# Merge gate projections by seven block products in place of eight

## The chip, the cores and the metric

One core of one Trainium2 chip runs the kernel. The metric is the device time of one execution in microseconds (us). Arithmetic is in float32; every large matmul is made of three, since both operands are split into a high part (float32r) and the rest: high by high, low by high, high by low.

## The reference

Two layers over 512 tokens of width 1024 (H is the normed input of 512 x 1024). Each layer projects H by one wide matrix, feeds four token mixers, gates them and merges them:

```python
merge = merge_in.reshape(B, T, N_BRANCH, D_MODEL)
...
    branch = (o * jax.nn.silu(gates[:, :, i])) @ w_branch[i]
    term = jax.nn.sigmoid(merge[:, :, i]) * branch
    acc = term if acc is None else acc + term
return x + acc @ w_out
```

merge_in is H times a 1024 x 4096 slice of the input weights: four 1024 x 1024 gate matrices, one per branch i.

## The kernel before

Tensors lie feature-major: 128 features on partitions, 512 tokens along the free dimension. `dense` (L224) makes one projection of 128 output features: 24 matmuls, for eight input blocks k of 128 features and three operand parts, with a 128 x 128 piece of weights as the stationary operand and 512 tokens as the moving one, into one of three PSUM banks named d. Its result is taken out of PSUM by a small generator that joins the list `bg` and is stepped on at every second matmul.

Weights come through the class `Stream` (L84) in one fixed order, 80 tiles of 128 x 1024 (512 KB) per layer. SP issues the loads into three buffers wr; `Stream.split` (L112) makes the high part on ACT (L69) into wh and the low part on DVE (L70) into wl, two buffers each, one tile ahead of the matmuls. A buffer wr is loaded again as soon as it is split.

A layer goes in these stages. First the key, query and value projections (`v_group`, L476, has tokens as rows: a block of H is stationary there and 400 columns of weights move). Then the eight branch gates (`GATES`, SiLU on ACT, L863), with the compressed-key work between. Then attention: 12 `Unit`s (L569), each of four score blocks S (L585, L586, softmax L588 to L600), transposes T (L609) and products PV (L630), written out by hand over 57 steps s (L920, L921). `FILL` = 7 matmuls of a filler (L890) are traced at each step: 16 projections of 24 matmuls, the last four being the merge gates of output block 0. Then the merge, eight output blocks m of 128 features (L942): for each, four dense projections give the gate logits of the four branches (L258 multiplies by the token's 1/rms, L749 takes tanh of half of it, since sigmoid(z) = (1 + tanh(z/2))/2), and `branches` (L753) makes four products of six matmuls (L764) into banks s and pt, multiplies by 1 + tanh (L769), adds (L773) and splits the sum (L72, L73) as a moving operand for the output projection. At last eight dense projections by w_out (L956 adds the residual; in the second layer they are made in two token halves of 256, L979).

The order in which an engine works is not the source order alone: Tile's scheduler takes, for each engine, the instruction that its own time model says is ready, with the source order as the priority, and allots buffers by tag (t: 8, st: 20, y: 16, p: 5, ptc: 2, V: 1) as they come free. The order so made is fixed in the program; each engine then runs its list in order.

## Time and profile before

| | |
|---|---|
| median of 3 runs | 974.78 us (974.34 to 974.78) |
| profiled execution | 972.54 us |
| its span, first to last instruction | 970.8 us |
| TensorE busy | 951.2 us, 98% of the span |
| VectorE (DVE) busy | 654.9 us, 67% |
| ScalarE (ACT) busy | 460.7 us, 47% |
| DMA traffic | 100.61 MB, mean 104 GB/s |

PE is TensorE's matmuls, DVE is VectorE, ACT is ScalarE, SP the queue that issues most DMAs. A matmul's record is longer than its share of the engine, since matmuls are pipelined: the pace is read from starts that follow each other. A row with "x96" is that many instructions merged. Releaser names after "<-" say what ended an idle time.

### The profile page before, as it was taken

What the parts mean: (1) busy time and instruction counts of PE and PEld (TensorE: products, weight loads), DVE (VectorE), ACT (ScalarE), POOL (GpSimd) and SP (SyncE); (2) the same over time, 40 slices, a digit from 0 to 9 for tenths busy, and PEclk for the clock granted to TensorE, in tenths of its full rate; (3) what the DMA queues carried; (4) which work ended last, traced back from release to release, by engine and by line L of the source; (5) the groups of instructions that cost most, each with busy time, mean ns of one, the idle gap of its engine ahead of it and who ended that gap; (6) DMA issues with size and microseconds to landing.
All of it is one profiled execution on the core that took longest, in us unless ns stands there. A gap on an engine that the chain in (4) does not pass through costs nothing.

```text
span 970.8 us, 12716 instructions
## 1 busy us (share of the span) xinstructions
PE 951.2 (98%) x4792; PEld 809.7 (83%) x4792; DVE 654.9 (67%) x1297; ACT 460.7 (47%) x816; POOL 17.2 (2%) x29
## 2 busy tenths in 40 slices
PE   7999999999999999999999999999999999999996
PEld 5988888888878888888889888888887888888896
DVE  6695699978775555446668549998779544555565
ACT  7384575666533232323426637566654332323363
POOL 0000000000000000000100000000000000000011
PEclk9999999999999999999999999999999999999998
DMA  6253232131122322335424322221210323232553
GB/s 264 76 177 106 87 98 66 56 98 51 59 86 89 100 97 92 103 111 182 163 66 155 130 87 86 67 69 62 66 65 23 129 87 109 87 109 87 185 185 129
DMA packets 31836, 100.61 MB, mean 104 GB/s; under 512 B 3600, under 2 KB 5664, under 8 KB 31776
## 3 DMA queue, kind: packets, MB, share of 16 engines
q1 hardware_dynamic: 30240, 96.65, 30.3%
q0 software_dynamic: 672, 2.11, 0.5%
q10 hardware_dynamic: 864, 1.05, 0.3%
q8 instruction: 37, 0.61, 0.3%
q14 instruction: 23, 0.19, 0.1%
HBM read 95.60 MB, written 4.19 MB: 103 GB/s over the span
## 4 chain that ended last, share of the span: by engine, by line
PE 96%; DVE 2%; ACT 0%; DMA 0%; issue 0%; POOL 0%; DVEq 0%; ACTq 0%; POOLq 0%
PE ps_d L237 73%; PE ps_s L764 4%; PE ps_pt L764 4%; PE ps_o L630 3%; PE ps_pt L609 3%; PE ps_s L488 2%; PE ps_pt L488 2%; PE ps_s L586 2%; PE ps_s L585 1%; PE ps_o L349 1%; DVE t L769 1%; DMA ng<-in_gains_dram 0%; PE ps_o L171 0%; PE ps_o L473 0%; PE ps_o L199 0%
## 5 line engine op out<-in xcount | busy, mean ns | idle before, releaser
L237 PE MATMUL ps_d<-xh,wh 128*128 128x512 f32 x888 | 349.1, 393 | 7.6 <-ACT xh L72 6.7
L237 PE MATMUL ps_d<-xl,wh 128*128 128x512 f32 x888 | 348.9, 393 | 0.0
L69 ACT ACTIVATE wh<-wr 128x1024 fp32r<-128x1024 f32 (+2 forms) x160 | 166.7, 1044 | 329.6 <-issue 221.3
L237 PE MATMUL ps_d<-xh,wl 128*128 128x512 f32 x888 | 241.2, 391 | 0.0
L70 DVE TENSOR_TENSOR wl<-wr,wh 128x1024 fp32r<-128x1024 f32 (+2 forms) x160 | 192.7, 1205 | 54.2 <-ACT wh L69 44.5
L237 PEld LDWEIGHTS ps_d<-xh,wh 128*128 128x128 f32 x888 | 167.5, 189 | 41.1 <-ACT xh L72 6.7
L237 PEld LDWEIGHTS ps_d<-xl,wh 128*128 128x128 f32 x888 | 167.3, 188 | 34.0 <-DVE xl L73 1.2
L237 PEld LDWEIGHTS ps_d<-xh,wl 128*128 128x128 f32 x888 | 165.7, 188 | 33.2
L258 DVE TENSOR_TENSOR t<-ps_d,rstd 128x512 f32<-128x512 f32 x106 | 73.0, 688 | 153.5 <-PE ps_d L237 153.0
L237 PE MATMUL ps_d<-st,wh 128*128 128x256 f32 (+1 forms) x384 | 67.6, 319 | 0.8 <-ACT wh L69 0.8
L590 ACT ACTIVATE p<-p,nm 128x128 f32<-128x128 f32 (+1 forms) x96 | 53.3, 556 | 31.1 <-DVE nm L588 30.8
L237 PEld LDWEIGHTS ps_d<-st,wh 128*128 128x128 f32 x384 | 57.1, 190 | 6.1 <-ACT wh L69 1.0
L588 DVE CUSTOM_DVE_ANT_0 p<-ps_s,cst 128x128 f32<-128x128 f32 (+1 forms) x96 | 45.4, 485 | 14.3 <-PE ps_s L586 9.1
L69 ACT ACTIVATE pth<-ps_pt 128x384 fp32r<-128x384 f32 (+1 forms) x72 | 37.1, 522 | 27.1 <-PE ps_pt L609 13.2
L70 DVE TENSOR_TENSOR ptl<-ps_pt,pth 128x384 fp32r<-128x384 f32 (+1 forms) x72 | 42.3, 596 | 2.7 <-ACT pth L69 2.6
L609 PE MATMUL ps_pt<-cst,p 128*128 128x128 f32 x240 | 40.8, 276 | 1.9 <-DVE ptl L70 1.2
L764 PE MATMUL ps_pt<-y,wh 128*128 128x512 f32 x128 | 41.6, 391 | 0.0
L764 PE MATMUL ps_s<-y,wh 128*128 128x512 f32 x128 | 40.8, 396 | 0.6 <-DVE y L643 0.6
L749 ACT ACTIVATE t<-t 128x512 f32<-128x512 f32 x64 | 39.4, 615 | 1.7 <-DVE t L258 1.5
L237 PE MATMUL ps_d<-st,wl 128*128 128x256 f32 (+1 forms) x192 | 37.9, 319 | 0.0
L630 PE MATMUL ps_o<-pth,V 128*128 128x256 f32 x144 | 37.3, 275 | 0.4 <-DVE o L654 0.4
L630 PE MATMUL ps_o<-ptl,V 128*128 128x256 f32 x144 | 36.1, 292 | 0.6 <-DVE ptl L70 0.6
(230 smaller groups left out, 1080.5 us busy)
## 6 DMA issues: line engine op xcount, KB each, us to landing
wr<-in_w_all_dram SPq DMA_DIRECT2D x159, 512.0 KB, 3.3
t<-in_xT_dram SPq DMA_DIRECT2D x16, 256.0 KB, 4.1
wr<-in_w_all_dram SPq DMA_DIRECT2D x8, 400.0 KB, 3.0
x1d<-t POOLq DMA_DIRECT2D x8, 256.0 KB, 2.3
xh<-x1d SPq DMA_DIRECT2D x8, 256.0 KB, 5.4
out_dram<-xh SPq DMA_DIRECT2D x12, 128.0 KB, 4.5
par<-in_par_dram SPq DMA_DIRECT2D x2, 279.5 KB, 4.7
wr<-in_w_all_dram ACTq DMA_DIRECT2D x2, 256.0 KB, 4.1
```

The costliest lines, as they stand in the source:

```text
L69: ACT.activation(hi, src, AF.Copy)
L70: DVE.tensor_tensor(lo, src, f32(hi), ALU.subtract)
L237: PE.matmul(acc[:, :width], w, r[k][:, tok], start=(n == 0), stop=(n == 23))
L258: DVE.tensor_tensor(t, acc, state["rb"], ALU.mult)
L488: PE.matmul(accs[tt][:, 0:400], x[:, tt * 128:tt * 128 + 128], w, start=(k == 0 and a == 0), stop=(kp == 3 and kk == 1 and a == 2))
L586: PE.matmul(s[:, :n], q2[:, c], kl[:, :n], start=False, stop=True)
L588: DVE.tensor_tensor_reduce(out=P[:, :n], in0=s[:, :n], in1=bias, scale=1.0, scalar=3e38, op0=ALU.add, op1=ALU.min, accum_out=nm)
L590: ACT.activation(P[:, :n], P[:, :n], AF.Exp, bias=nm, scale=-1.0, accum_out=sm)
L609: PE.transpose(p[:, c:c + 128], self.P[qt][:, kb * 128:kb * 128 + 128], ident)
L630: PE.matmul(dst, V[:, kb, self.vset, :], part[:, src], start=(self.fresh and self.cmp is None and b == 0 and kb == 0 and j == 0), stop=(se ...
L749: ACT.activation(t, t, AF.Tanh, scale=0.5)
L764: PE.matmul(p, w[:, c], r, start=(n == 0), stop=(n == 5))
```

## The change

The 512 x 1024 H is cut into two halves of tokens and two of input features, the gate weights of two branches (one half fh of 512 output features) into two halves of input features and the two branches. That 2 x 2 by 2 x 2 block product is made by seven products of sums and differences of blocks (P1 to P7, Strassen's scheme in Winograd's form) in place of eight. Each product is of 256 tokens by 512 input features by 512 output features: two halves h, two token blocks tt, two blocks kk, three parts, so 24 matmuls, now with a 128 x 128 block of H stationary and 512 weight columns moving. There are four such blocks per layer (fh, bp). The 1/rms goes into the tanh as a scale per partition, since tokens are rows now. P1, P6, P5 and P3 add up in banks X (d), P7 and P4 in W (s), P2 in Y (pt); partial sums are copied out of X by ACT between the products.

`combine_h` makes the sums of the blocks of H from the layer's input, loaded again; six of its 24 pieces are traced in the last attention steps, the rest ahead of the first P7. `prepare` makes the sums of the weight tiles on DVE and splits them; T2 is kept from P7 to P4. The stream now loads 80 merge tiles per layer (18 + 2 in each block, some twice) in place of 40, and has seven slots in the merge (three wr, the rope tables' buffer, three in V's buffer) in place of three. Sets of split weights rotate over wh/wl (two) and the buffers of the attention transposes (one), so three sets. The branch products have tokens as rows too. The merged sum of a half fh is transposed back by 16 PE transposes and split. Four of the eight SiLU gates move into the filler, made by tanh, in the place of the four merge gates; the compressed-key work moves from the gate stage to the attention's head; the filler is spread evenly over all 57 steps in place of 7 per step.

The diff, cut to its core (removed: `ev_merge`, `branches` and the loop over m, printed above; cut here too: buffer renames and the packing of the weights on the host):

```diff
-FILL = 7
 HID = (9, 11, 13, 15)
-GATES = [(0, 0), (2, 0), (0, 1), (2, 1), (1, 0), (3, 0), (1, 1), (3, 1)]
+GATES = [(0, 0), (2, 0), (0, 1), (2, 1)]
+GATES2 = [(1, 0), (1, 1), (3, 0), (3, 1)]
 BIG = 1e30
 HEAD_ROWS = (1, 3, 0, 2)
 SWAP = [(i + 8) % 16 if i < 16 else i for i in range(32)]
@@ -81,40 +82,85 @@
...
 
+
+    PRODUCTS = ("P1", "P2", "P7", "P6", "P5", "P3", "P4")
+
+    NEEDS = {"P1": (0,), "P2": (2,), "P7": (3, 1), "P6": (0,), "P5": (1, 0), "P3": (3,), "P4": (2,)}
...
-            self.order = [(l, i) for l in range(L) for i in range(NTILE)]
+            self.order = []
+            for l in range(L):
+                self.order += [(l, i) for i in range(MERGE0)]
+                for b in range(4):
+                    o = MERGE0 + 10 * b
+                    for name in PRODUCTS:
+                        self.order += [(l, o + 2 * q + h) for h in range(2) for q in NEEDS[name]]
+                    self.order += [(l, o + 9), (l, o + 8)]
+                self.order += [(l, i) for i in range(NTILE - KT, NTILE)]
...
+            self.slots = ["wr"] * 3
...
+    def combine_h(l):
+
+        src = xT.rearrange("(k p) t -> k p t", p=128) if l == 0 else x1d
+        H = T // 2
+        S = state["S"] = {n: [] for n in ("P7", "P6", "P5", "P3")}
+        lo_, hi_ = slice(0, H), slice(H, T)
+        keep = []
+        for k in range(4):
+            xa = [sb([128, T], "ptc", 2) for _ in range(2)]
+            for n in range(2):
+                nc.sync.dma_start(xa[n], src[k + 4 * n])
+            if k % 2 == 0:
...
+            yield
...
+            for n in range(2):
+                ACT.activation(xa[n], xa[n], AF.Copy, scale=ng[:, 8 * l + k + 4 * n:8 * l + k + 4 * n + 1])
+            yield
+            c = k % 2
...
+            DVE.tensor_tensor(tmp[:, 0], xa[0][:, lo_], xa[0][:, hi_], ALU.subtract)
+            DVE.tensor_tensor(s1[:, c], xa[0][:, hi_], xa[1][:, hi_], ALU.add)
+            parts("P7", tmp[:, 0])
+            yield
+            DVE.tensor_tensor(tmp[:, 1], s1[:, c], xa[0][:, lo_], ALU.subtract)
+            parts("P6", tmp[:, 1])
+            yield
+            s4 = xa[1][:, lo_]
+            DVE.tensor_tensor(s4, s4, tmp[:, 1], ALU.subtract)
+            parts("P3", s4)
+            yield
...
+        for k in range(4):
+            h, lo = xh[k][:, hi_], xl[k][:, hi_]
+            split(h, lo, keep[k // 2][:, k % 2])
+            S["P5"].append((h, lo))
+            yield
...
+    def prepare():
...
+        def parts(r):
+            if next(count) % 3 == 2:
+                hi, lo = (sb([128, 2, T], "ptx", 2, F32R).rearrange("p a b -> p (a b)") for _ in range(2))
             else:
...
+                hi, lo = sb([128, 1024], "wh", 2, F32R), sb([128, 1024], "wl", 2, F32R)
+            split(hi, lo, r)
+            ready.append((hi, lo))
...
+        for blk in range(4):
+            t2 = [None, None]
+            for name in PRODUCTS:
+                for h in range(2):
+                    r, slot = t2[h] if name == "P6" else ws.next_raw()
+                    if name in ("P7", "P5", "P6"):
+                        b, other = ws.next_raw()
+                        DVE.tensor_tensor(r, r, b, ALU.add if name == "P6" else ALU.subtract)
+                        ws.free(other)
+                        yield
+                    elif name == "P4":
+                        b, other = t2[h]
+                        DVE.tensor_tensor(r, r, b, ALU.subtract)
+                        ws.free(other)
+                        yield
+                    parts(r)
+                    if name in ("P7", "P6"):
+                        t2[h] = r, slot
+                    else:
+                        ws.free(slot)
+                    yield "ready"
...
+
+        rth = sb([128, 4], "rth", 1)
+        DVE.tensor_scalar(rth, state["rt"], 0.5, None, op0=ALU.mult)
+        big = sb([128, 3, 1024], "V", 1)
+        ws.slots += ["rope"] + [big[:, n] for n in range(3)]
+        ws.fill()
...
+        for fh in range(2):
+            acc = [None] * 4
+            for bp in range(2):
+                X = Y = W = None
+                sig = {}
+                s1, u2, u4 = [None] * 2, [None] * 2, [None] * 2
+                for name in PRODUCTS:
+                    if name == "P1":
+                        X = [psum("d", 3) for _ in range(2)]
+                    elif name == "P2":
+                        Y = [psum("pt", 2) for _ in range(2)]
+                    elif name == "P7":
+                        run(side)
+                        W = [psum("s", 2) for _ in range(2)]
+                    bank = Y if name == "P2" else W if name in ("P7", "P4") else X
+                    opens = name in ("P1", "P2", "P7")
+                    for h in range(2):
+                        wh, wl = take_ready()
+                        for tt in range(2):
+                            for kk in range(2):
+                                k = 2 * h + kk
+                                a, b = rows(name, k, tt)
+                                d = slice(kk * 512, kk * 512 + 512)
+                                for n, (x, w) in enumerate(((a, wh), (b, wh), (a, wl))):
+                                    PE.matmul(bank[tt], x, w[:, d], start=(opens and k == 0 and n == 0),
+                                              stop=(name in ("P2", "P3", "P4") and k == 3 and n == 2),
+                                              skip_group_check=True)
+                            if h == 0 and tt == 0:
+                                merge_ahead(2)
+                        merge_ahead(2)
+                    for tt in range(2):
+                        if name in ("P1", "P6", "P5"):
+                            t = sb([128, T], "p", 5) if name == "P5" and bp == 0 else temp()
+                            ACT.activation(t, X[tt], AF.Copy)
+                            {"P1": s1, "P6": u2, "P5": u4}[name][tt] = t
+                        if name == "P2":
+                            DVE.tensor_tensor(s1[tt], Y[tt], s1[tt], ALU.add)
+                            tanh(s1[tt], s1[tt], tt)
+                            sig[0, tt] = s1[tt]
+                        elif name == "P5":
+                            DVE.tensor_tensor(u4[tt], W[tt], u4[tt], ALU.add)
+                            tanh(u4[tt], u4[tt], 2 + tt)
+                            sig[1, 2 + tt] = u4[tt]
+                        elif name == "P3":
+                            t = temp() if bp else sb([128, T], "p", 5)
+                            tanh(t, X[tt], tt)
+                            sig[1, tt] = t
+                        elif name == "P4":
+                            DVE.tensor_tensor(u2[tt], W[tt], u2[tt], ALU.add)
+                            tanh(u2[tt], u2[tt], 2 + tt)
+                            sig[0, 2 + tt] = u2[tt]
...
+                banks = itertools.cycle((("pt", 2), ("o", 1), ("pt", 2), ("d", 3)))
+                for j, toks in ((1, (2, 3, 0, 1)), (0, (0, 1, 2, 3))):
+                    wh, wl = take_ready()
+                    for tok in toks:
+                        p = psum(*next(banks))
+                        n = 0
+                        for kt in range(2):
+                            yh, yl = state["y"][2 * bp + j, kt]
+                            c, d = slice(tok * 128, tok * 128 + 128), slice(kt * 512, kt * 512 + 512)
+                            for x, w in ((yh, wh), (yl, wh), (yh, wl)):
+                                PE.matmul(p, x[:, c], w[:, d], start=(n == 0), stop=(n == 5))
+                                n += 1
+                        sg = sig[j, tok]
+                        DVE.scalar_tensor_tensor(sg, sg, 1.0, p, op0=ALU.add, op1=ALU.mult)
+                        if acc[tok] is None:
+                            acc[tok] = sg
+                        else:
+                            DVE.tensor_tensor(acc[tok], acc[tok], sg, ALU.add)
+                        if tok == toks[0]:
+                            merge_ahead(2)
+
...
+            for f in range(4):
+                pt = psum("pt", 2)
+                for tok in range(4):
+                    PE.transpose(pt[:, tok * 128:tok * 128 + 128], acc[tok][:, f * 128:f * 128 + 128], ident)
+                tag = (("st", 20), ("y", 16))[fh]
+                h, lo = sb([128, T], *tag, F32R), sb([128, T], *tag, F32R)
+                split(h, lo, pt, scale=0.5)
+                ah[4 * fh + f], al[4 * fh + f] = h, lo
...
+        def ev_gate_tanh(i, f):
+
+            def g(acc):
+                t, gt = temp(), temp()
+                DVE.scalar_tensor_tensor(t, acc, 0.5, state["rb"], op0=ALU.mult, op1=ALU.mult)
+                yield
+                ACT.activation(gt, t, AF.Tanh)
+                yield
+                DVE.scalar_tensor_tensor(gt, gt, 1.0, t, op0=ALU.add, op1=ALU.mult)
+                state["gate"][i, f] = gt
+                yield
+            return g
...
         for n, (i, f) in enumerate(GATES):
-            run_with(dense(rhs, ev_gate(i, f)), ch if n > 4 else None, 3)
-            if n < 4:
-                hd = hidden(n // 2, n % 2)
...
+            run(dense(rhs, ev_gate(i, f)))
+            hd = hidden(n // 2, n % 2)
+            next(hd)
+            bg.insert(0, hd)
...
+            for i, f in GATES2:
+                yield from dense(rhs, ev_gate_tanh(i, f))
...
-            for i in range(4):
-                yield from dense(rhs, ev_merge(i))
...
-        side = itertools.chain(decay(l), cmp_attention())
-        for n in range(48):
+        side = itertools.chain(cmp_k(), cmp_v(), decay(l), cmp_attention())
...
+        left = 16 * 24 - 60
...
                                     pump_bg(1)
                         getattr(units[u], kind)(b)
-            for _ in range(FILL):
+            n = -(-left // (steps - s))
+            left -= n
+            for _ in range(n):
                 next(fill, None)
+            if s == 44:
+                combos = combine_h(l)
+            if combos is not None and s % 2:
+                next(combos, None)
+        run(fill)
...
-        for m in range(KT):
-            if m:
-                for i in range(4):
...
-            a, b = branches(m)
-            ah.append(a)
-            al.append(b)
+
+        ah, al = merge(l, combos)
```

## Rows read from the trace of the kernel before

**Rows 1.** The page: busy time, DVE and clock in 40 slices, chain that ended last.

```profile
PE 951.2 (98%) x4792; PEld 809.7 (83%) x4792; DVE 654.9 (67%) x1297; ACT 460.7 (47%) x816; POOL 17.2 (2%) x29
...
PEclk9999999999999999999999999999999999999998
...
PE 96%; DVE 2%; ACT 0%; DMA 0%; issue 0%; POOL 0%; DVEq 0%; ACTq 0%; POOLq 0%
```

**Rows 2.** Windows of layer 0: merge (m = 0 to 5), attention's tail, attention, merge's end, start.

```profile
core 0: us, PE busy (x) PEld busy (x) DVE busy (x) ACT busy (x) POOL busy (x), PEclk, DMA share, GB/s
275.30:438.80 163.50, 163.50 (x721) 135.41 (x722) 87.12 (x109) 48.70 (x62) 0.00 (x0) 1.00 0.32 103
257.00:275.30 18.30, 16.17 (x84) 12.58 (x83) 15.94 (x29) 7.88 (x16) 0.00 (x0) 1.00 0.09 30
96.00:257.00 161.00, 161.00 (x867) 138.40 (x866) 133.26 (x341) 99.16 (x207) 2.13 (x4) 1.00 0.23 74
438.80:466.00 27.20, 27.20 (x121) 22.52 (x121) 15.34 (x20) 10.36 (x15) 2.23 (x4) 1.00 0.51 181
0.00:20.00 20.00, 13.30 (x49) 10.15 (x50) 13.18 (x25) 14.82 (x24) 0.94 (x5) 1.00 0.83 318
```

**Rows 3.** Chain of waits, one merge block: start us, us, what.

```profile
302.79 21.76 PE ps_d L237 x96
```

**Rows 4.** Timeline of PE: transposes of one attention unit, start us, us.

```profile
140.05 0.60 PE L609 MATMUL ps_pt<-cst,p 128*128 128x128 f32 x4
```

**Rows 5.** Groups of the attention's tail, 257.05 to 275.28 us, on PE.

```profile
L764 PE MATMUL ps_s<-y,wh 128*128 128x512 f32 x16 | 5.5, 413 | 0.3 <-DVE y L643 0.3
L764 PE MATMUL ps_pt<-y,wh 128*128 128x512 f32 x16 | 5.1, 397 | 0.0
L764 PE MATMUL ps_s<-y,wl 128*128 128x512 f32 x8 | 3.1, 392 | 0.0
L764 PE MATMUL ps_pt<-y,wl 128*128 128x512 f32 x8 | 3.1, 391 | 0.0
L630 PE MATMUL ps_o<-ptl,V 128*128 128x256 f32 x8 | 2.4, 305 | 0.6 <-DVE ptl L70 0.6
L630 PE MATMUL ps_o<-pth,V 128*128 128x256 f32 x8 | 2.3, 301 | 0.3 <-DVE o L654 0.3
L609 PE MATMUL ps_pt<-cst,p 128*128 128x128 f32 x10 | 1.6, 277 | 0.6 <-DVE ptl L70 0.6
```

**Rows 6.** Groups by form, whole span: weight splits, evacuations, tanh, sums.

```profile
L70 DVE TENSOR_TENSOR wl<-wr,wh 128x1024 fp32r<-128x1024 f32 x150 | 183.4, 1223 | 45.6 <-ACT wh L69 40.4 <-PE ps_o L199 4.4
...
L69 ACT ACTIVATE wh<-wr 128x1024 fp32r<-128x1024 f32 x150 | 158.5, 1059 | 311.8 <-issue 218.3 <-PE ps_d L237 85.8 <-PE ps_s L764 3.5
L258 DVE TENSOR_TENSOR t<-ps_d,rstd 128x512 f32<-128x512 f32 x106 | 73.0, 688 | 153.5 <-PE ps_d L237 153.0
...
L749 ACT ACTIVATE t<-t 128x512 f32<-128x512 f32 x64 | 39.4, 615 | 1.7 <-DVE t L258 1.5
L773 DVE TENSOR_TENSOR t<-t 128x512 f32<-128x512 f32 x48 | 33.1, 689 | 0.9
...
L70 DVE TENSOR_TENSOR st<-wr,st 128x256 fp32r<-128x256 f32 x32 | 11.7, 420 | 2.7 <-ACT st L69 2.7
...
L73 DVE SCALAR_TENSOR_TENSOR st<-t,st 128x512 fp32r<-128x512 f32 x16 | 11.1, 693 | 9.0 <-ACT st L72 8.8
...
L72 ACT ACTIVATE st<-t 128x512 fp32r<-128x512 f32 x16 | 10.1, 633 | 29.5 <-DVE t L773 29.5
```

**Rows 7.** Timeline of DVE at a merge block's end: start us, us.

```profile
303.74 1.23 DVE L70 TENSOR_TENSOR wl<-wr,wh 128x1024 fp32r<-128x1024 f32 x1
304.88 0.68 DVE L773 TENSOR_TENSOR t<-t 128x512 f32<-128x512 f32 x1
306.26 0.69 DVE L73 SCALAR_TENSOR_TENSOR st<-t,st 128x512 fp32r<-128x512 f32 x1 [0.70 <-ACT st L72]
```

**Rows 8.** DMA issues by line: KB each, median us to landing.

```profile
wr<-in_w_all_dram SPq DMA_DIRECT2D x159, 512.0 KB, 3.3
t<-in_xT_dram SPq DMA_DIRECT2D x16, 256.0 KB, 4.1
...
xh<-x1d SPq DMA_DIRECT2D x8, 256.0 KB, 5.4
```

**Rows 9.** Timeline of SP in layer 0's merge: issues (start us, us).

```profile
424.68 5.77 SPq L109 DMA_DIRECT2D wr<-in_w_all_dram  x2
430.49 0.90 SPq L965 DMA_DIRECT2D t<-in_xT_dram  x2
435.65 5.67 SPq L109 DMA_DIRECT2D wr<-in_w_all_dram  x2
```

More of the change, by code (lines that the diff above doesn't have):

```diff
@@ new lines, in merge_ahead, with take_ready, merge, tanh @@
+    def merge_ahead(n=1):
+        if state.get("prep") is None:
+            state["prep"] = prepare()
+        end = object()
+        while len(ready) < n and next(state["prep"], end) is not end:
+            pass
+    def take_ready():
+        merge_ahead(1)
+        return ready.pop(0)
+    def merge(l, side):
+        rth = sb([128, 4], "rth", 1)
[3 more added lines that the diff above has]
+        ws.fill()
+        ah, al = [None] * KT, [None] * KT
+        def tanh(dst, src, tok):
+            ACT.activation(dst, src, AF.Tanh, scale=rth[:, tok:tok + 1])
+        for fh in range(2):
[5 more added lines that the diff above has]
+                for name in PRODUCTS:
+                    if name == "P1":
+                        X = [psum("d", 3) for _ in range(2)]
[57 more added lines that the diff above has]
+                            acc[tok] = sg
+                        else:
+                            DVE.tensor_tensor(acc[tok], acc[tok], sg, ALU.add)
[9 more added lines that the diff above has]
+                ah[4 * fh + f], al[4 * fh + f] = h, lo
+        state["prep"] = None
+        assert not ready
+        return ah, al
```

145 lines of the change are left out of this document (84 added, 61 removed).

## The prediction

> **What bounds the kernel now.** I read four views in this order. The page first: TensorE is busy 98% of the span, its granted clock is at the upper level (2.4 GHz) nearly all the time, and the chain that ended last is PE for 96% [rows 1]. So time can only be gained by giving PE fewer columns, or lost by making it wait. Then the windows by stage: through six merge blocks of layer 0 PE is busy 163.50 of 163.50 us, while DVE has 87.12 and ACT 48.70, so the stage that changes is PE's alone and DVE is half idle; attention is different, with DVE at 133.26 of 161.00; and in attention's tail PE is idle for 2.13 of 18.30 us [rows 2]. Third the chain inside one merge block: 96 matmuls of 512 columns in 21.76 us, nothing between, so one costs 0.2267 us [rows 3]. Last the DMA share of the merge, 0.32 [rows 2].
>
> A change of 0.2% (2 us) is about what a measurement of this kernel can tell from none. Durations are those of the profiled execution, 972.54 us (span 970.8), and the sum is made against it; the median of the runs is 974.78, 2.24 more, which I add at the end.
>
> **The change part by part.**
> *Products.* Before, 32 merge projections of 24 matmuls per layer, 768. After, four blocks of seven products of 24, 672. The branch products stay 192. So 96 fewer per layer, 192 in all: 192 x 0.2267 = **-43.5 us**. What is stationary and what moves is exchanged, but both shapes stay 128x128 and 512 columns, so I keep the pace.
> *Transposes.* New: 2 x 16 per layer. Four of attention's take 0.60 us with a last record of 0.27, so 0.11 each [rows 4]; 64 x 0.11 = **+7.0** (up to 64 x 0.27 = 17 if nothing overlaps). PE's own bill is therefore -36.5.
> *Filler spread over 57 steps, gates in place of merge gates in it.* The count of matmuls stays 384. Today the filler is used up before the last steps: in the tail PE has 48 matmuls of 512 columns (10.9 us) and 34 small ones of about 0.11 (3.7) in 18.2 us, so 3.6 us per layer are lost [rows 5]. Spread, it covers part of that: I take 2 per layer, **-4** (0 to -7). The compressed-key steps that move to attention's head have 60 filler matmuls (13.6 us) beside them and more to come; they cost nothing unless DVE is late there.
> *DVE in the merge.* Per layer 64 weight splits in place of 40, and 32 new sums of weight tiles of the same shape: 96 x 1.223 = 117.4 us [rows 6]. Of 128x512 operations at 0.69 [rows 6] there are 24 PSUM sums, 32 gate products, 24 sums and 8 splits: 60.7 (the 32 multiplications by 1/rms are gone). That is 178 us of records. Neighbours overlap: a split of 1.23 us begins at 303.74, the next operation at 304.88, 0.09 before the split's record ends [rows 7], and a window counts that once. With 0.09 off each of the 184 operations DVE has 161.5 us beside 864 x 0.2267 + 3.5 = 199.4 of PE: 81%, against 53% before (14.5 of 27.2 per block). Outside the merge DVE gets 32 operations of 128x256 for the sums of H (0.42 each [rows 6], 13.4 us) and 4 x 0.69 for the gates. What that costs PE is bounded by two rows: at 83% (133.26 of 161.00) PE shows no idle time, at 87% (15.94 of 18.30) it is idle 12% of the time [rows 2]. The second stretch has little independent PE work, the merge has a lot and three sets of split weights, so I stay near the first: 2.5% of 199, **+10** for both layers (0 to 46).
> The Trainium skill ("VectorE: DVE Perf Modes", Terms) says of this that a pipeline flush follows each DVE operation and that the next can't issue until the pipe is empty; taken at its word nothing would overlap, the term would be 46 and the time 988 (rival E), while the records in the trace do overlap.
> *Handing X on.* P6 and P5 end with a copy of X by ACT, and the next product adds to the same banks. Each bank has six matmuls of the other token block as cover, 1.36 us; the copy is 0.62 and may stand behind one weight split of 1.06 [rows 6]: 1.68, so up to 0.32 is open. 16 such places, I take 0.2 each: **+3** (0 to 5).
> *Start and end of the merge.* V's buffer gives three of the seven slots only after the last PV; two tiles must land (3.3 us [rows 8]), be summed and split (1.22 + 1.06 + 1.22) before P7: 6.8 us, beside P1 and P2 (48 x 0.2267 = 10.9). Hidden. At the end the last gate product, the sum (2 x 0.69), four transposes (0.44), ACT's high part 0.63 and DVE's low part 0.69 stand before the fifth input block of the output projection: 3.1 us, against eight matmuls on the first four blocks, 1.8. 1.3 open, and DVE is behind there; I take 2.5 per layer, **+5** (0 to 20).
> *ACT.* 64 x 1.06 + 56 x 0.62 + 8 x 0.63 = 108 us of 199 in the merge, plus 11 for H's sums. Not a bound.
> *DMA.* 80 tiles instead of 40 per layer: 512 KB per 2.49 us, 210 GB/s, at the share of 0.32 for five tiles per 27.2 us about 0.70 of the engines. The trace shows 318 GB/s at 0.83 in its first 20 us and 181 at 0.51 with PE never idle [rows 2]. Zero on average. Per slot: two of the seven hold T2 from P7 to P4, so five turn over. They need 1.43 tiles per half product of 2.72 us, so a turn may last 9.5 us; it needs landing 3.3 (5.4 for the slowest kind of row [rows 8]) and 3.5 of sum and split, 6.8 to 8.9. SP waits in order, so a late slot holds back the loads behind it.
>
> Sum: -43.5 + 7.0 - 4 + 10 + 3 + 5 = -22.5. 972.54 - 22.5 = 950.0; as a median **952 us**.
>
> **The rivals.**
> *A, nothing is given back:* the terms for DVE, X and the ends are zero and the tail gives 7: 972.54 - 43.5 = 929, 931 as a median. For it: half a DVE is idle in the merge now. Against: 81% afterwards, and the tail shows what chains through DVE cost.
> *B, the sums of H are late.* Three of four rounds are traced ahead of the first P7, with two buffers ptc: a load of 4.1 us [rows 8], two scalings by ACT (1.2), seven DVE operations (2.9), 8.2 per round, one load already done: 20.5 us against P1, P2 and half of P7, 13.6. 7 us per layer, 14 in all: 966. Against it: the order is not the source's alone. The residual loads (L965), traced after the whole merge, are issued at 430.49 between merge loads [rows 9], so rounds can start early as well.
> *C, slower: the chain sum, high part, low part of one weight set bounds each half product that needs a sum.* Place: 8 of 14 half products in each of 8 blocks. If DVE's sum, ACT's split and DVE's split follow each other with nothing of the next set between, they take 1.22 + 1.06 + 1.22 = 3.5 us against 2.72 of PE: 0.78 x 64 = +50 in place of the 10: 992. It decides from 0.51 us per such step, where the 33 us left without it are gone. For it: DVE already waits 40.4 us for ACT's high part before the low part [rows 6], and what is queued behind it on DVE, PSUM's evacuation, waits too. Against: three sets, and the scheduler can put other work into that wait. The Trainium skill ("TensorE: Matmul & The Clock Gate", Architectural detail) calls ACT and DVE strict first in, first out, and this is the way in which such a queue would give 992; the wait of DVE's split on ACT in the trace agrees with it.
> *D, slower: slots.* If a slot's turn is 1 us over the 9.5, 3.6 turns per block in 8 blocks add 29: 981.
> *E, slower: DVE's operations don't overlap where shapes change.* 178 of 199 us is 89%, past the tail's 87%; with its 12% idle, 46 in place of 10: 988. Against: [rows 7] show an overlap between two unlike operations.
> That the change does less than it says I leave out: the seven products can be counted in the diff.
>
> **How the numbers follow.** Forecast 0.63, its own range 938 to 967 (from tail -7, DVE 2 and X 0 to DVE 25). A 0.10, B 0.10, C 0.12, D 0.03, E 0.02. Faster: forecast, A and B less 0.01, 0.82. Slower: 0.15 of C, D and E; 0.03 for a B or C that ends on the old time. The range, 936 to 980, takes in B and half-sized C, and leaves out most of A and the full C, D and E.
>
> **What the profile would show.** PE has 192 fewer matmuls of 512 columns and 64 more transposes; the pace stays 0.227. DVE rises from 655 to about 800 us, ACT from 461 to about 560, DMA from 101 to about 147 MB. Merge windows of one layer near 205 us with DVE at 75 to 85% and PE idle for some per cent, just after P6 and P5 and at a block's end. In the tail PE has filler to the end. Wrong would be: PE idle in the P7, P6, P5 and P4 half products with releaser DVE (C), or with a DMA (D); one gap of several us before the first P7 of a layer (B); a granted clock at the lower level (1.2 GHz) in the merge, which no term holds; or a longer pace with H stationary.

## The result: 4.7% slower, and the profile after

The changed kernel takes 1019.57 us as the median of four runs (1017.3 to 1025.13), the kernel before 974.56 (974.16 to 974.78). The ratio is 1.0471, with a 95% interval of 1.0429 to 1.0513. 952 was forecast, 980 was the top of the range, so the forecast was wrong and so was its sign. The four runs spread over 7.8 us, so what hangs on their median is known to a few us only.

The page of the changed kernel (profiled execution of 1019.55 us, span 1017.8), the lines that answer to [rows 1]:

```profile
PE 955.2 (94%) x4664; PEld 792.7 (78%) x4664; DVE 789.8 (78%) x1467; ACT 561.9 (55%) x960; POOL 17.1 (2%) x29
...
PEclk9999999986999999999999999999779999999998
DMA  7153222223757565553515313112157575666353
...
DMA packets 45664, 146.77 MB, mean 144 GB/s; under 512 B 5136, under 2 KB 7200, under 8 KB 45600
...
PE 68%; DVE 18%; DMA 7%; issue 4%; ACT 2%; DVEq 0%; SPq 0%; POOL 0%; ACTq 0%; POOLq 0%
```

The saved work is there: 4664 records on PE in place of 4792, which is 192 fewer and 64 more. Yet PE is busy longer than before: a matmul's record lasts about 0.39 us where the pace is 0.2267, so a short pause between matmuls, or a lower clock, counts as busy. And the chain that ended last is no longer PE's alone: DVE has 18% of it and DMA 7%. In two places, one per layer, the granted clock falls. The windows of layer 0 show which stage that is (same columns as [rows 2]):

```profile
core 0: us, PE busy (x) PEld busy (x) DVE busy (x) ACT busy (x) POOL busy (x), PEclk, DMA share, GB/s
105.00:194.00 89.00, 89.00 (x466) 75.90 (x465) 78.88 (x200) 55.89 (x115) 1.56 (x3) 1.00 0.22 72
194.00:248.00 54.00, 44.96 (x227) 35.29 (x226) 51.74 (x161) 43.08 (x105) 0.52 (x1) 0.80 0.25 73
248.00:300.00 52.00, 49.62 (x206) 38.96 (x207) 42.34 (x49) 26.75 (x35) 0.00 (x0) 0.98 0.72 237
300.00:350.00 50.00, 48.40 (x211) 39.11 (x211) 39.34 (x44) 24.03 (x30) 0.00 (x0) 1.00 0.64 200
350.00:400.00 50.00, 44.88 (x200) 35.41 (x199) 36.40 (x40) 25.84 (x33) 0.00 (x0) 1.00 0.60 187
400.00:462.00 62.00, 60.06 (x262) 48.23 (x261) 50.16 (x60) 26.47 (x33) 0.00 (x0) 1.00 0.50 160
```

The same two attention windows of the kernel before:

```profile
105.00:194.00 89.00, 89.00 (x469) 76.03 (x469) 80.11 (x196) 57.03 (x114) 1.61 (x3) 1.00 0.23 72
194.00:248.00 54.00, 54.00 (x307) 46.95 (x305) 42.11 (x116) 33.05 (x75) 0.52 (x1) 1.00 0.23 74
```

Up to 194 us the two kernels are alike. From 194 to 248, still attention, PE went from 54.00 busy to 44.96, DVE from 42.11 to 51.74 of 54.00 (96%), and the clock from 1.00 to 0.80. After that comes the merge, where PE idles 11.04 of 214 us and DVE is busy for 168.24 of them (79%); before it idled in none of it [rows 2]. So there are two holes, one of them in a stage where the change was thought to help.

What PE does in the first hole is read from its groups. The kernel before, 105 to 194 and then 194 to 248, matmuls of `dense`:

```profile
L237 PE MATMUL ps_d<-xl,wh 128*128 128x512 f32 x96 | 38.0, 396 | 0.0
L237 PE MATMUL ps_d<-xh,wh 128*128 128x512 f32 x95 | 37.7, 396 | 0.0
L237 PE MATMUL ps_d<-xh,wl 128*128 128x512 f32 x89 | 24.8, 390 | 0.0
...
L237 PE MATMUL ps_d<-xh,wh 128*128 128x512 f32 x49 | 19.4, 397 | 0.0
L237 PE MATMUL ps_d<-xl,wh 128*128 128x512 f32 x49 | 19.2, 392 | 0.0
L237 PE MATMUL ps_d<-xh,wl 128*128 128x512 f32 x56 | 15.5, 394 | 0.0
L609 PE MATMUL ps_pt<-cst,p 128*128 128x128 f32 x50 | 8.6, 277 | 0.0
```

The changed kernel in the same two windows:

```profile
L283 PE MATMUL ps_d<-xh,wh 128*128 128x512 f32 x96 | 37.9, 394 | 1.0 <-ACT wh L70 1.0
L283 PE MATMUL ps_d<-xl,wh 128*128 128x512 f32 x96 | 37.8, 393 | 0.0
L283 PE MATMUL ps_d<-xh,wl 128*128 128x512 f32 x96 | 27.0, 393 | 0.0
...
L656 PE MATMUL ps_pt<-cst,p 128*128 128x128 f32 x67 | 14.8, 329 | 4.8 <-DVE ptx L71 3.7 <-DVE p L647 1.1
L632 PE MATMUL ps_s<-st 128*128 128x384 f32 (+3 forms) x22 | 9.5, 434 | 2.7 <-DVE nm L635 2.7
```

Before, 280 dense matmuls run in the first window and 154 in the second: 434, more than the 384 of the whole filler. The rest are merge projections of the next output block, which the scheduler had pulled forward. By 258 us the kernel before has issued eight tanh of L749, those of blocks 0 and 1. In the changed kernel 288 run in the first window at the same rate, and none but one at the edge in the second: the filler is used up at 194 us, 54 us ahead of attention's end. What is left there are the 24 matmuls of P1 and attention's own chain, which waits for DVE at the transposes and at the scores. Attention itself is not longer for it: the last PV product of layer 0 starts at 247.4 us, and at 268.4 before. What is lost is the work that ran beside it.

### The profile page after: what moved, and what is told of

Same layout as the page of the kernel before. It is cut to its first block, busy times and chain, and to the rows that moved or that the text cites. A ratio compares the mean times of both kernels' runs of the same rounds, so it can differ in the third digit from the quotient of the medians.

```text
span 1017.8 us, 13052 instructions
## 1 busy us (share of the span) xinstructions
PE 955.2 (94%) x4664; PEld 792.7 (78%) x4664; DVE 789.8 (78%) x1467; ACT 561.9 (55%) x960; POOL 17.1 (2%) x29
## 2 busy tenths in 40 slices
DMA packets 45664, 146.77 MB, mean 144 GB/s; under 512 B 5136, under 2 KB 7200, under 8 KB 45600
## 4 chain that ended last, share of the span: by engine, by line
PE 68%; DVE 18%; DMA 7%; issue 4%; ACT 2%; DVEq 0%; SPq 0%; POOL 0%; ACTq 0%; POOLq 0%
PE ps_d L283 35%; PE ps_d L940 14%; DMA V<-in_w_all_dram 4%; DVE wl L71 3%; PE ps_s L940 3%; DVE ptx L71 3%; PE ps_pt L978 2%; PE ps_o L678 2%; PE ps_s L534 2%; PE ps_pt L534 2%; DMA wr<-in_w_all_dram 2%; PE ps_pt L656 1%; DVE p L635 1%; DVE V L872 1%; PE ps_o L978 1%
## 5 line engine op out<-in xcount | busy, mean ns | idle before, releaser
L71 DVE TENSOR_TENSOR wl<-wr,wh 128x1024 fp32r<-128x1024 f32 (+2 forms) x124 | 148.2, 1198 | 53.9 <-ACT wh L70 50.7
L283 PE MATMUL ps_d<-xh,wh 128*128 128x512 f32 x376 | 148.8, 397 | 8.4 <-ACT xh L73 6.9
L283 PE MATMUL ps_d<-xl,wh 128*128 128x512 f32 x376 | 149.3, 398 | 0.0
L283 PE MATMUL ps_d<-xh,wl 128*128 128x512 f32 x376 | 104.7, 393 | 0.0
L283 PEld LDWEIGHTS ps_d<-xh,wh 128*128 128x128 f32 x376 | 71.4, 190 | 22.3 <-ACT xh L73 6.9
L283 PEld LDWEIGHTS ps_d<-xl,wh 128*128 128x128 f32 x376 | 71.3, 190 | 14.5 <-DVE xl L74 1.2
L283 PEld LDWEIGHTS ps_d<-xh,wl 128*128 128x128 f32 x376 | 69.5, 188 | 13.8
L678 PE MATMUL ps_o<-ptx,V 128*128 128x256 f32 (+1 forms) x288 | 57.7, 324 | 3.2 <-DVE ptx L71 1.2
L678 PEld LDWEIGHTS ps_o<-ptx,V 128*128 128x128 f32 x288 | 48.0, 222 | 10.8 <-DVE ptx L71 3.8
L940 PE MATMUL ps_d<-wh,st 128*128 128x512 f32 x176 | 53.1, 392 | 1.6 <-ACT wh L70 1.4
L70 ACT ACTIVATE ptx<-ps_pt 128x384 fp32r<-128x384 f32 (+1 forms) x72 | 37.1, 518 | 15.1 <-PE ps_pt L656 11.6
L940 PEld LDWEIGHTS ps_d<-wh,st 128*128 128x128 f32 x176 | 32.8, 188 | 9.4 <-ACT wh L70 2.9
```

The lines of the kernel that those rows point to most:

```text
L70: ACT.activation(hi, src, AF.Copy)
L71: DVE.tensor_tensor(lo, src, f32(hi), ALU.subtract)
L283: PE.matmul(acc[:, :width], w, r[k][:, tok], start=(n == 0), stop=(n == 23))
L678: PE.matmul(dst, V[:, kb, self.vset, :], part[:, src], start=(self.fresh and self.cmp is None and b == 0 and kb == 0 and j == 0), stop=(se ...
L940: PE.matmul(bank[tt], x, w[:, d], start=(opens and k == 0 and n == 0), stop=(name in ("P2", "P3", "P4") and k == 3 and n == 2), skip_group ...
```

## The experiments

Three theories stood at the start, with these numbers in the expectations. T1: attention's new side (four SiLU gates in the filler where merge gates had been, compressed-key work moved, filler spread) leaves attention without cover. T2: the chain sum, high part, low part of the weights bounds the merge. T3: the sums of H take DVE's time at attention's end. Kernels run together share runs of the kernel before on their chip, so each time is also given as its distance to those: the change itself is at +45.0. e1 to e7, h1 and h2 are one run each, beside one run of the kernel before (e7 beside 17, which spread over 3.6 us), so differences of less than about 4 us say little.

**e1: attention's new side, with the old merge of eight products.**

```diff
-            for i in range(4):
-                yield from dense(rhs, ev_merge(i))
+            for i, f in GATES2:
+                yield from dense(rhs, ev_gate_tanh(i, f))
...
-            if m:
-                for i in range(4):
-                    run(dense(rhs, ev_merge(i)))
+            for i in range(4):
+                run(dense(rhs, ev_merge(i)))
```

> The kernel before with the change's attention side alone: four SiLU gates in the filler (by tanh), compressed-key steps in attention's head, filler spread evenly, all merge gates after attention; the merge stays in eight direct products. Theory 1 (cover): attention's first score is pinned at about 105 us by the compressed-key chain, the filler covers that wait now and runs out early, and the attention's second half is DVE alone with PE idle: 988 to 1005 us. Theory 2 (the seven-product merge itself, its weight sums and loads) and theory 3 (the sums of H on DVE): no part of either is in here, 970 to 980 us.

Measured 976.71, +4.0, in the range of theories 2 and 3. Moving the gates and the compressed keys costs little as long as the old merge follows. T1 as first put was wrong; the next run says the same from the other side.

**e2: the changed kernel with the old eight gates ahead of attention and a filler of twelve projections.**

```diff
+GATES = [(0, 0), (2, 0), (0, 1), (2, 1), (1, 0), (3, 0), (1, 1), (3, 1)]
...
-        left = 16 * 24 - 60
+        left = 12 * 24 - 48
```

> The changed kernel with the front of before: eight SiLU gates ahead of attention, compressed-key steps among them, filler of twelve projections (no gates, no merge gates), spread evenly. Theory 1: attention starts at the same time with about 45 matmuls more in hand (10 us per layer): 995 to 1008 us. Theories 2 and 3: 1013 to 1023 us.

Measured 1023.72, +51.0, just over the range of theories 2 and 3: no help.

**e3: the changed kernel without the sums of H** (it leaves them out; the products that need them take parts of H as they are).

```diff
-        for k in range(4):
...
-            DVE.tensor_tensor(tmp[:, 0], xa[0][:, lo_], xa[0][:, hi_], ALU.subtract)
...
+        state["S"] = {n: [(xh[k][:, :T // 2], xl[k][:, :T // 2]) for k in range(4)] for n in ("P7", "P6", "P5", "P3")}
```

> The changed kernel without the sums of H: the products P7, P6, P5 and P3 read blocks of H itself; nothing is loaded again, scaled, added or split for them. Theory 3 (these operations, 13 us of DVE and 11 of ACT per layer, stand in the stretch that DVE bounds, and delay its chains beyond their own time): 965 to 985 us. Theory 1 (they add their own DVE time to a stretch that is long for want of cover): 990 to 1008 us. Theory 2: 1012 to 1020 us.

Measured 998.25, +25.5: the sums of H cost 45.0 - 25.5 = 19.5 us. Theory 3 had said 965 to 985; the time lies in theory 1's range.

**e4: the changed kernel without the 32 sums of weight tiles per layer** (it leaves them out; loads and splits stay).

```diff
-                        DVE.tensor_tensor(r, r, b, ALU.add if name == "P6" else ALU.subtract)
...
-                        DVE.tensor_tensor(r, r, b, ALU.subtract)
```

> The changed kernel without the sums of weight tiles on DVE (32 per layer, 39 us); all tiles are still loaded, split and multiplied. Theory 2 (DVE sums bound the merge): 975 to 990 us, with PE idle in the merge below 3 us per layer. Theory 1: the stretch from 194 to 248 us stays and only part of the merge's 16 us per layer goes: 995 to 1012 us.

Measured 990.93, +18.2, at the edge of theory 2's range: the sums cost 26.8 us. In layer 0 what they cost lies in the merge, not in attention, as the windows of e4 show; DVE is as full in the first as it was:

```profile
194.00:248.00 54.00, 44.82 (x229) 36.26 (x228) 51.10 (x156) 42.18 (x102) 0.52 (x1) 0.81 0.32 99
...
250.00:440.00 190.00, 186.26 (x818) 151.02 (x818) 125.46 (x146) 100.98 (x129) 0.00 (x0) 1.00 0.63 207
```

T2 and T3 are both causes, and neither alone gives back the old time. What no run had yet closed is the hole from 194 to 248, at 9.18 us in e4 and 6.73 in e3. So T1 was put anew, as **theory 1'**: attention goes at DVE's pace and PE idles unless independent matmuls stand beside it. Before, merge projections of later blocks were such work: they need only H, a wh/wl pair and a bank d. The seven products can't stand in: the third weight set lies in attention's ptx buffers, P2 and P7 use its banks pt and s, weights wait for V's buffer, and P7 for the sums of H. The first split into ptx comes just as attention's last PV product lets the buffer go (timeline of DVE, changed kernel):

```profile
247.87 1.23 DVE L71 TENSOR_TENSOR ptx<-wr,ptx 128x1024 fp32r<-128x1024 f32 x1 [0.72 <-PE ps_o L678]
```

**e5: as e4, and without the second tile's load** (14 tiles per block in place of 18).

```diff
-    NEEDS = {"P1": (0,), "P2": (2,), "P7": (3, 1), "P6": (0,), "P5": (1, 0), "P3": (3,), "P4": (2,)}
+    NEEDS = {"P1": (0,), "P2": (2,), "P7": (3,), "P6": (), "P5": (1,), "P3": (3,), "P4": (2,)}
```

> As the kernel without weight sums (990.93 us), and without the loads that only the sums need: 14 tiles per block in place of 20; each product multiplies one loaded tile. If DVE's sums alone held the merge back, the loads are hidden and this is the same, 986 to 995 us. If the turn of the seven slots (landing 4.2 us under load, DVE's release, SP in order) holds what is left of the merge's idle time (9 us per layer), 970 to 982 us.

Measured 987.03, +12.5, as expected if the loads are hidden. The loads beyond the old number, slots included, are worth 5.7 us at most once the sums are gone (3.9 by the times themselves), which single runs hardly tell from nothing.

**e6: the changed kernel with the weight sums on POOL.**

```diff
-                        DVE.tensor_tensor(r, r, b, ALU.add if name == "P6" else ALU.subtract)
+                        POOL.tensor_tensor(r, r, b, ALU.add if name == "P6" else ALU.subtract)
```

> The changed kernel with the 32 weight sums per layer on POOL in place of DVE; result unchanged. If DVE's busy time holds the merge back: as without the sums, 988 to 1000 us. If the length of the chain landing, sum, split does (a 128x256 operation took POOL 0.82 us before, so about 3.3 for 128x1024 against 1.2 on DVE): 1015 us and more. The attention's loss stays in both.

Measured 1036.07, +61.6, worse than with the sums on DVE. The timeline of POOL, then of DVE, e6:

```profile
320.35 2.38 POOL L872 TENSOR_TENSOR V<-V,rope 128x1024 f32<-128x1024 f32 x1 [0.96 <-DMA rope<-in_w_all_dram]
...
320.51 3.30 DVE L71 TENSOR_TENSOR ptx<-wr,ptx 128x1024 fp32r<-128x1024 f32 x1
```

A split that takes 1.22 us by itself begins 0.16 after a sum on POOL and ends 1.08 after it: it stood still while POOL worked. The split before it, begun at 318.16 within a sum of POOL that ends at 319.39, lasts 2.32 and ends 1.09 after that. The Trainium skill ("SBUF — State Buffer", Who interferes with whom) has this as a rule: a VectorE instruction with two SBUF inputs contends with a GpSimd instruction that reads SBUF, and the later one is blocked until the other ends. This trace agrees, with 3.30 against 1.22.

**h1: half of each.** Blocks 0 to 3 of a layer as before, with the old filler and its merge gates; blocks 4 to 7 by two seven-product blocks, with the sums of H beside the first half.

```diff
-                for b in range(4):
+                for b in range(2):
...
+        for m in range(4):
+            if m:
+                for i in range(4):
+                    run_with(dense(rhs, ev_merge(i)), early, 12)
```

> A mix: output blocks 0 to 3 by eight direct products with the front, the filler and the four merge gates in it as before, and blocks 4 to 7 by two blocks of seven products per layer; the sums of H are made beside the direct blocks. Theory 1 as it stands now (attention is DVE's, and the direct merge gates are the PE work that can run beside it, which the seven products cannot): attention's loss is that of before, 13 us per layer; each seven-product block gains 4.6 us on PE and loses 5.5 waiting: 972 to 984 us. If the merge's waits come from its start behind attention alone: 956 to 968 us. If the seven products cost attention in some other way: over 995 us.

Measured 974.07, -0.4. From 194 to 248 PE is busy 54.00 of 54.00 again: with merge gates of the old kind behind attention the first hole is closed. What two seven-product blocks save per layer goes into waits: from 275 to 440 us PE idles 4.87 of 165, where before it idled 0.29.

**h2: h1 with the weight sums on POOL.** The edit is that of e6.

> The mix with the weight sums on POOL. If DVE's sums make the wait of a seven-product block (5.5 us down to about 2.5, as without the sums): 960 to 971 us, faster than before. If POOL's longer chain makes it worse: 980 us and more.

Measured 989.3, +14.8: as in e6, the sums on POOL cost more than those on DVE.

**e7: the changed kernel with six dummy projections at the filler's end.**

```diff
+            for _ in range(6):
+                acc = psum("d", 3)
+                for n in range(24):
+                    PE.matmul(acc, xh[n // 3][:, :128], xh[n // 3], start=(n == 0), stop=(n == 23))
+                    yield
```

> The changed kernel with six more filler projections per layer that use no weights and whose results go nowhere: 144 more matmuls of 512 columns per layer, 144 x 0.2267 = 32.6 us of PE per layer, 65.3 in all, added at the end of attention's filler. Theory 1' (PE is idle beside attention because attention goes at DVE's pace and the filler is used up) expects 1015 to 1035 us, most of the 65 us disappearing in the idle time. The rival, that PE's own work bounds this stretch as well, or that the dummies delay the chain by taking PE's turn, expects 1055 to 1085.

Measured 1058.23, +85.2: 40.2 more than the changed kernel for 65.3 us of matmuls. That is in the rival's range; theory 1', with 1015 to 1035, missed. The window of e7 and the one behind it:

```profile
194.00:248.00 54.00, 54.00 (x301) 46.54 (x300) 38.06 (x118) 27.41 (x69) 0.52 (x1) 1.00 0.15 45
248.00:300.00 52.00, 46.28 (x191) 35.80 (x190) 44.16 (x76) 33.56 (x60) 0.00 (x0) 0.84 0.61 199
```

In the first PE has no idle time left and the clock is at the upper level throughout, while DVE falls from 51.74 to 38.06: with 32.6 us of cover per layer PE bounds this stretch once more. But that also delays attention, as the rival said: its last PV product starts at 263.5 us in place of 247.4, and behind 248 us PE idles 5.72 of 52 at a clock of 0.84. So the hole was partly filled and partly pushed back, and of 65.3 us of matmuls about 65.3 - 40.2 = 25 were free over both layers. Theory 1' had the mechanism and took the hole for larger than the dummies.

**h3a: h1 with the low-part matmuls later in each half product**, so that the last split of a set has more cover.

```diff
+                        todo = [(tt, kk, n) for tt in range(2) for n in (0, 1) for kk in range(2)]
+                        if h:
+                            todo = [(tt, kk, n) for tt in range(2) for g in ((0, 1), (2,)) for kk in range(2) for n in g]
+                        else:
+                            todo += [(tt, kk, 2) for tt in range(2) for kk in range(2)]
```

> The half-way kernel (blocks 0 to 3 of each layer with eight products, 4 to 7 with seven), with the low-part weight matmuls placed later in each half product, so that the last split of a weight set has 1.8 us more of cover. If the Strassen blocks of the half-way kernel lose their time to weight parts that come too late, PE idles some 3 to 8 us less per layer and the time is 960 to 969. If they lose it to DVE's total load, it stays at 971 to 976.

Measured 972.1 (12 runs) against 973.06 (17 runs): ratio 0.9989, interval 0.9976 to 1.0001, not to be told from no change, as h1 is not either. So a gain by the late low part is not shown, and the time is in the range expected of DVE's total load. Its windows in attention's tail and the first half of the merge:

```profile
258.00:275.00 17.00, 15.96 (x84) 12.54 (x82) 14.70 (x29) 7.99 (x17) 0.00 (x0) 1.00 0.35 113
275.00:350.00 75.00, 72.68 (x320) 59.81 (x320) 59.08 (x90) 37.79 (x57) 0.00 (x0) 1.00 0.47 150
```

**h3: h3a with the loads of x for the sums of H in attention's ptx buffers**, so that they start only at its end.

```diff
-            xa = [sb([128, T], "ptc", 2) for _ in range(2)]
+            xb = sb([128, 2, T], "ptx", 2)
+            xa = [xb[:, 0], xb[:, 1]]
```

> As the kernel with the low parts later, and the loads of x for the sums of H go to buffers that attention holds until its end, so that these sums cannot be taken up in attention's tail and two rounds can be in flight. If sums of H taken up early are what makes the tail wait (1.6 us at y, and more behind it), 2 to 5 us less than the other: 957 to 966. If not, the same within 2 us, or later by the time that the loads now start later.

Measured 980.12, ratio 1.0063 (1.0048 to 1.0079): 8 us over h3a, where a gain was hoped for. Sums of H begun later cost more than those taken up in attention's tail; here they also hold buffers that the third weight set uses, and the two were not told apart.

Two kernels bear most on the main question. **e9: e1 with the first two merge projections in attention's accumulator bank o**, so that no merge projection can run beside attention. The work is that of e1; the diff is against e1.

```diff
+    def dense(rhs, evac, tok=slice(0, T), bank=("d", 3)):
...
-                run(dense(rhs, ev_merge(i)))
+                run(dense(rhs, ev_merge(i), bank=("o", 1) if m == 0 and i < 2 else ("d", 3)))
```

> The kernel with the change's attention side and the old eight-product merge (976.71 us), in which the first two merge projections take attention's own accumulator bank, so that no merge projection can run beside attention; the work is the same. If the lost cover is a cause by itself, attention is left with idle PE at its end, about 10 us per layer as in the changed kernel without sums of H, and the time is 990 to 1005 us. If cover is worth nothing and only the new DVE work counts, it stays at 975 to 982.

Measured 1011.57 against 973.89, +37.7, ratio 1.0394 (1.0379 to 1.041): 33.7 us more than e1, beyond what either theory gave and on the side of theory 1'. Windows of layer 0 and layer 1, first e1, then e9, with two of e9's waits from 194 to 262 us:

```profile
194.00:238.00 44.00, 44.00 (x251) 38.13 (x249) 35.81 (x99) 26.22 (x60) 0.52 (x1) 1.00 0.23 73
...
690.00:765.00 75.00, 72.83 (x385) 60.77 (x384) 57.41 (x131) 38.68 (x80) 0.00 (x0) 1.00 0.17 57
```

```profile
194.00:238.00 44.00, 33.59 (x200) 26.47 (x198) 41.62 (x136) 31.83 (x81) 0.52 (x1) 0.92 0.08 25
...
690.00:765.00 75.00, 66.30 (x321) 54.26 (x322) 52.50 (x139) 37.02 (x84) 0.00 (x0) 0.89 0.12 39
...
PE ps_o L237 <- DVE o L654: 1.4, 1, 1.4
PE ps_o L237 <- DVE t L258: 0.8, 1, 0.8
```

Without a single seven-product block, and with no more work (4792 matmuls in both, DVE busy 658.4 us against 658.1 in e1), the hole of the changed kernel appears: in layer 0 PE idles 10.41 of 44 us, DVE is 95% busy, the clock falls. In time of full clock that fall is up to (1 - 0.92) x 44 = 3.5 us in layer 0 and (1 - 0.89) x 75 = 8.3 in layer 1, about a third of the 33.7. The two waits on bank o are the price of the means, 2.2 us per layer.

**e8: the changed kernel without either kind of sums** (the edits of e3 and e4 together; it leaves both out).

> The changed kernel without the sums of H and without the sums of weight tiles (it leaves both out; splits, loads and products stay). If the two costs found singly, 1019.6 - 998.25 = 21 us and 1019.6 - 990.93 = 29 us, add up, it takes 965 to 975 us, and what is left over the forecast without any DVE cost is the lost cover and the handing over. If the two hide each other, 980 to 990; if nothing but DVE was the matter, 935 to 950.

Measured 975.19 against 973.89, ratio 1.0011 (0.9995 to 1.0026): within the noise the two costs add up, 43.7 us together against 19.5 + 26.8 = 46.3 singly. The window of e8:

```profile
194.00:248.00 54.00, 47.42 (x264) 38.53 (x263) 48.00 (x141) 36.85 (x88) 0.52 (x1) 0.94 0.26 83
```

Even with all its sums for nothing, and 192 matmuls fewer, the seven-product merge only draws level. The missing cover is the larger part of why, with PE idle for 6.58 us in this window, but not all of it, as the sum below shows.

## Why the prediction was wrong, step by step

**PE's own bill, -36.5: right.** The counts came out, and in the merge twelve matmuls still take 2.72 us, 0.227 each, with H stationary. What the products and the new transposes take beyond that is mostly waiting (chain of waits, changed kernel):

```profile
278.45 2.72 PE ps_d L940 x12
```

**The step that failed: the filler, "-4 (0 to -7)".** The prediction said "The count of matmuls stays 384". That is the count in the source, and it is not what ran beside attention. There the kernel before had 434 dense matmuls in the two windows, merge projections of block 1 among them, which the scheduler had pulled into a stage that, left to itself, goes at DVE's pace; the changed kernel had 288. Nor did spreading the filler over 57 steps reach the engine: with source order only as a priority it ran at the old rate and was out at 194 us, where "In the tail PE has filler to the end" had been forecast. So the tail of [rows 5], with 2.13 us of idle time [rows 2], grew to a stretch of 54 us with 9.04 idle and a lower clock. e9 measures what it is worth with nothing else changed in the merge, +33.7; with what e1 adds, attention's side is at +37.7 where -4 stood. In the changed kernel it is less, about +25 without any sums, as the sum below shows. The prediction had both facts in hand: DVE at 83% in attention with PE never idle [rows 2], and loads hoisted out of source order [rows 9]. It used the full PE there as a bound for the merge, and did not ask whose matmuls kept it full.

**Sums of H: put at nothing for attention.** Their 13.4 us of DVE were counted and laid outside the merge, with the remark on order for rival B only. In layer 0 they run from 207 to 257 us, most of that where DVE is the bound, and cost 19.5 (e3).

**DVE in the merge, "+10": right in kind, too small.** DVE's share was forecast at 81% and is 79% from 248 to 462. But the share does not set the price: e4 puts the sums alone at 26.8. The waits of PE in the changed kernel (us in total, times, longest):

```profile
PE ps_pt L656 <- DVE ptx L71: 7.9, 9, 1.4
PE ps_d L283 <- ACT xh L73: 6.9, 1, 6.9
PE ps_d L940 <- DVE wl L71: 6.9, 5, 1.6
PE ps_s L632 <- DVE nm L635: 5.9, 9, 1.3
PE ps_s L940 <- DVE wl L71: 4.5, 6, 1.6
```

In the merge (L940) PE waits for the low part, the last link of the chain that rival C named. One such wait, first DVE's timeline and then PE's:

```profile
306.05 1.23 DVE L872 TENSOR_TENSOR wr<-wr,rope 128x1024 f32<-128x1024 f32 x1
309.26 1.23 DVE L872 TENSOR_TENSOR V<-V 128x1024 f32<-128x1024 f32 x1 [1.98 <-DMA V<-in_w_all_dram]
310.40 1.22 DVE L71 TENSOR_TENSOR wl<-wr,wh 128x1024 fp32r<-128x1024 f32 x1
311.54 1.28 DVE L952 TENSOR_TENSOR t<-ps_pt,t 128x512 f32<-128x512 f32 x2
312.74 1.22 DVE L872 TENSOR_TENSOR wr<-wr 128x1024 f32<-128x1024 f32 x1
313.87 1.22 DVE L872 TENSOR_TENSOR V<-V,rope 128x1024 f32<-128x1024 f32 x1
315.00 1.22 DVE L71 TENSOR_TENSOR wl<-wr,wh 128x1024 fp32r<-128x1024 f32 x1
...
316.27 0.50 PE L940 MATMUL ps_d<-wl,st 128*128 128x512 f32 x1 [1.58 <-DVE wl L71]
```

DVE stands still for 1.98 us for a tile in a late slot (rival D's place), then has six operations to make up, three of them sums for later sets, and PE waits 1.58 for a split that is behind them. So C was half right: at 26.8 of its 50 us. D is small once the sums are gone, where loads and slots are worth 5.7 at most (e5); beside the sums no run prices it. B named the sums of H, but at the first P7, where e9 and e3 put the loss earlier. A is far off, and for E nothing speaks: DVE's operations still start 1.13 us apart at 1.22 each (313.87, 315.00). ACT and DMA cost what they were said to: DVE 789.8, ACT 561.9 and 146.77 MB against "about 800", "about 560" and "about 147".

**The sum.** By distances to the kernel before: -36.5 for PE's bill, +37.7 for attention's side (e9), +19.5 for the sums of H, +26.8 for the weight sums, less 46.3 - 43.7 = 2.6 counted twice: +44.9, against +45.0 measured; and -36.5 + 37.7 = +1.2 against +1.3 for e8. That they fit to 0.1 us is luck. e9 has no products beside attention, where the changed kernel has P1's 24, so it overstates the lost cover by up to 2 x 24 x 0.2267 = 10.9, and 4.4 of it is the waits on bank o. The traces allow a sum without differences of runs. The time from each matmul's start to the next one's, waits and slower clock included, added up by group over both layers (us):

| | before | e9 | changed | e3 | e4 | e8 | e7 |
|---|---|---|---|---|---|---|---|
| attention's own matmuls (S, T, PV) | 89.7 | 126.8 | 135.0 | 115.8 | 127.8 | 114.7 | 100.5 |
| the seven products, 304.7 at the pace | | | 337.7 | 335.3 | 319.5 | 317.7 | 344.1 |
| the 64 new transposes, 7.0 forecast | | | 13.8 | 13.0 | 10.0 | 10.0 | 13.2 |

So -43.5 for the products' count, +45.3 in attention, +33.0 in the seven products, +13.8 for the transposes and -1.7 in all the rest make +46.9; the spans differ by 47.0. Attention loses 25.0 without any sums (e8), the nearest that the runs give to the lost cover of this kernel alone, against 37.1 in e9; the sums of H add 19.2 (e3), and dummies beside it bring the 45.3 down to 10.8 (e7). The seven products lose 18.2 to the weight sums (e4), and 13.0 with no sums at all (e8), where 8 was forecast for handing X on and the merge's ends. Waits are put to the matmul before them; put to the one behind, no figure moves by more than 3 us. What those 13.0 are, no run took apart; more splits and loads than before are in them too.

The clock at the lower level was named as a sign of error, for the merge; it came in attention. PE had been busy without a break from 105 to 194 us at the upper level (2.4 GHz), then idled 9.04 of 54 us, and the granted clock over these is 0.80: as a mean of 1 and one half, 0.4 of them, about 22 us, at 1.2 GHz. Transposes last 329 ns there in place of 277. No term held this: up to (1 - 0.80) x 54 = 10.8 us in layer 0, and (1 - 0.84) x 75 = 12.0 in layer 1, whose window is:

```profile
690.00:765.00 75.00, 60.90 (x287) 46.77 (x285) 70.31 (x180) 52.38 (x118) 0.52 (x1) 0.84 0.35 114
```

Most of it is a part of the 45.3 above, not more on top. The Trainium skill ("TensorE: Matmul & The Clock Gate", What's actually happening) says that the clock has these two levels and that idleness brings the lower one; the trace agrees, and so does e7, in which the same stretch filled with dummies has 1.00 and the one behind it, with PE idle again, 0.84.

## What to carry to other kernels

A stage in which PE is full can still be another engine's stage: look at which of PE's matmuls there belong to it and which are cover drawn from elsewhere, counted on the engine and not in the source, before changing the stage that the cover comes from. Of a form with fewer products ask whether its operands can be made ready wherever the old form's could; here it needs DVE for every sum and buffers that the stage before still holds. Where one engine prepares operands in order, its share of busy time says little: price the chain of sum, high part and low part with the oldest unrelated operation queued in front.

## What was not expected of the hardware

A DVE operation with two inputs in SBUF did not slow a little beside POOL, it stopped for as long as POOL's own lasted (3.30 us in place of 1.22, e6), and POOL takes about 2.4 us for a sum that DVE makes in 1.22. So POOL's idle 98% was no reserve for these sums: moving them cost about 1036.07 - 1019.57 = 16.5 us.

No kernel here beats the kernel before by more than the noise. The best, h3a, does with half the seven-product blocks what the kernel before does without any.
